# Residues of the MLP input's weights: an accumulating DMA onto the negated rounded half in place of VectorE subtractions

## The chip, the cores and the metric

The kernel runs on one core of a Trainium2 chip. The metric is device time in microseconds of one execution, as the median of several runs. A difference of 0.2% (about 4.5 us) is what a measurement of this kernel can tell from no change.

## The reference, cut to what matters

A trunk of two layers over 256 tokens of width 2048. Each layer has attention (differential and neighbourhood heads) and then a squared-ReLU MLP with 8192 hidden columns. All is float32. The change is in the weights of the first MLP product:

```python
h = rmsnorm(x, mlp_norm[l])
u = jax.nn.relu(jnp.einsum('bsd,df->bsf', h, w_mlp_in[l]))
x = x + jnp.einsum('bsf,fd->bsd', u * u, w_mlp_out[l])
```

## The kernel before, in words

**Split weights.** TensorE multiplies rounded operands (float32r). To keep float32's accuracy, every weight is split into a rounded half and a residue, w = hi + lo with hi = round(w) and lo = w - hi, and so is every activation. A product is then three matmuls into one accumulator: hi x hi, hi x (activation's residue), and lo x hi. The lo half is used by the third alone.

**Slabs.** All weights are packed on the host into slabs of 128 x 2048 floats (1 MB), 192 for each layer, 384 in all, in the order of use. `next_slab` loads one into `raw` (three buffers, on SP's DMA queue, in program order) and splits it in two halves of 128 x 1024: ScalarE (ACT) copies to `whi` (line 130), VectorE (DVE) subtracts to `wlo` (line 131). Each of `whi` and `wlo` has four buffers, which all products of the kernel share.

**Who uses a slab.** `block_product` has the weights as the moving operand, 24 matmuls of 512 columns for each slab (the attention's input, the output projection, the MLP's output: lines 153 to 155). `stationary_product` has the weights as the stationary operand, 48 matmuls of 256 columns for each slab (lines 180 to 182, accumulator `accu`). It serves the neighbourhood heads' q and k (16 slabs a layer, 32 in all) and the MLP's input (64 slabs a layer, 128 in all).

**The MLP.** The hidden columns go in four chunks (`N_CHUNK`). A chunk is an input stage of 16 slabs (`F_PER_CHUNK`), each followed by `rl` = relu (ACT, line 524), `u` = accu x rl (DVE, line 526) and the split of u into `u2T` (ACT line 136, DVE line 137); and then an output stage of 16 slabs, four blocks of four. Two layers make eight such chunks.

**What sets the order.** Each engine runs its instructions in a fixed order, which a scheduler writes from a timeline of its own when the kernel is built; only the loads on SP's queue keep the program's order. What an engine does ahead of TensorE is bounded by the buffers of `raw`, `whi` and `wlo`. GpSimd (POOL) does small things: the scales of the norms (lines 189, 191), the rotary sums (line 250), the biases. It issues no DMA.

Of the kernel before, what the change touches and what calls it, by code (L numbers as in the profile page):

```python
# [11 lines left out]
F32 = mybir.dt.float32  # L12
F32R = mybir.dt.float32r
AF = mybir.ActivationFunctionType
ALU = mybir.AluOpType
# [20 lines left out]
NB = 512  # L36
NEG = -1.0e30
RUN = 5 * RPB_C + GRID_W
# Where a query of column 0 and an even row finds its last neighbour in a head's reversed table.
RPB_FIRST = RPB_HEAD - 1 - (10 * RPB_C + GRID_W - 1 + WIN_C - 1)  # L40
N_CHUNK = 4
F_PER_CHUNK = D_FF // P // N_CHUNK
SLABS = 48 + 16 + 64 + 64
# Column blocks of 512 of the input projection: q, k, v of the differential heads 0-3, then 4-7.
DIFF_BLOCKS = [0, 2, 4, 1, 3, 5]
NA_Q, NA_K, NA_V = 3 * HALF, 4 * HALF, 5 * HALF

# [1 line left out]
def body(ctx, tc, x, x_t, w, gains_in, gains_o, final_g, lam_in, rpb, ident_in, rope_in, mask_in, out):  # L49
# [5 lines left out]
    small = ctx.enter_context(tc.tile_pool(name="small", bufs=4))  # L55
    ps = ctx.enter_context(tc.tile_pool(name="ps", bufs=2, space=PSUM))

# [1 line left out]
    gin = const.tile([P, 2 * DEPTH, NK], F32, name="gin")  # L59
    nc.scalar.dma_start(gin, gains_in)  # L60
    ident = const.tile([P, P], F32, name="ident")
# [3 lines left out]
    xs = [const.tile([P, D], F32, name=f"x{t}") for t in range(NT)]  # L65

    def stream(dst, src):
        """A load on the queue of the weights, in the order of the program."""
        tc.keep_in_program_order(nc.sync.dma_start(dst, src))

    lam_sb = [None]

    def load_table(l):
        """The relative position biases of a layer, from where each query reads its windows."""
        table = act.tile([P, HEADS, RUN + 1], F32, name="table", tag="table", bufs=1)
        for rr in range(P // GRID_W):
            src = bass.AP(tensor=rpb.tensor,
                          offset=rpb.offset + l * HEADS * RPB_HEAD + RPB_FIRST + rr * RPB_C,
                          ap=[[1, GRID_W], [RPB_HEAD, HEADS], [1, RUN]])
            stream(table[rr * GRID_W:(rr + 1) * GRID_W, :, :RUN], src)  # L80
        return table
# [23 lines left out]
    ones = const.tile([P, P], F32, name="ones")  # L105
    nc.vector.memset(ones, 1.0)

# [1 line left out]
    slab_no = [0]  # L109
    x_rest = [None]  # L110

    def next_slab():
        i = slab_no[0]
        slab_no[0] += 1
        raw = wp.tile([P, 2048], F32, name="raw", tag="raw", bufs=3)
        if i == 0:
            for c in range(0, 2048, NB):
                if c == NB:
                    x_rest[0]()
                stream(raw[:, c:c + NB], w[i, :, c:c + NB])  # L120
        else:
            stream(raw, w[i])
        parts = []
        for h in range(2):
            hi = wp.tile([P, 1024], F32R, name="whi", tag="whi", bufs=4)
            lo = wp.tile([P, 1024], F32R, name="wlo", tag="wlo", bufs=4)
            step = NB if i == 0 else 1024
            for c in range(0, 1024, step):
                r = raw[:, h * 1024 + c:h * 1024 + c + step]
                nc.scalar.activation(hi[:, c:c + step], r, AF.Copy)  # L130
                nc.vector.tensor_sub(lo[:, c:c + step], r, hi[:, c:c + step].bitcast(F32))  # L131
            parts.append((hi, lo))
        return parts

# [3 lines left out]
                                       op0=ALU.mult, op1=ALU.subtract)  # L138

    def block_product(n_k, operand, before=None, split_tail=0):  # L140
        """[256, 512] = sum over n_k blocks of 128 of operand(k)^T @ the next slabs. The last
        `split_tail` slabs are held together, so that one tile of tokens ends before the other."""
        acc = [ps.tile([P, NB], F32, name="acc", tag="acc", bufs=4) for _ in range(NT)]
        parts = []
        todo = []

        def one(k, t):
            hi, lo = parts[k // 2]
            c0 = (k % 2) * NB
            a = operand(k)  # L150
            wh, wl = hi[:, c0:c0 + NB], lo[:, c0:c0 + NB]
            ah, al = a[:, 0, t * P:(t + 1) * P], a[:, 1, t * P:(t + 1) * P]
            nc.tensor.matmul(acc[t], ah, wh, start=k == 0, stop=False)  # L153
            nc.tensor.matmul(acc[t], al, wh, start=False, stop=False)  # L154
            nc.tensor.matmul(acc[t], ah, wl, start=False, stop=k == n_k - 1)  # L155

        n_s = n_k // 4
        for s in range(n_s):
            if before is not None:
                before(s)  # L160
            parts += next_slab()
            todo += range(4 * s, 4 * s + 4)
            if s < n_s - split_tail:
                for k in todo:
                    for t in range(NT):
                        one(k, t)
                todo = []
        for t in range(NT):
            for k in todo:
                one(k, t)  # L170
        return acc

    def stationary_product(h_t):
        """[128, 256] = the next slab^T @ normed activations, transposed."""
        parts = next_slab()
        acc = ps.tile([P, S], F32, name="accu", tag="acc", bufs=4)
        for k in range(NK):
            hi, lo = parts[k // 8]
            wh, wl = hi[:, (k % 8) * P:(k % 8 + 1) * P], lo[:, (k % 8) * P:(k % 8 + 1) * P]
            nc.tensor.matmul(acc, wh, h_t[k][:, 0], start=k == 0, stop=False)  # L180
            nc.tensor.matmul(acc, wh, h_t[k][:, 1], start=False, stop=False)  # L181
            nc.tensor.matmul(acc, wl, h_t[k][:, 0], start=False, stop=k == NK - 1)  # L182
        return acc

# [1 line left out]
    def rms_scale(ss, n, width):  # L186
        """(ss / width + EPS) ** -0.5 on [128, n]."""
        v = small.tile([P, n], F32, name="v")
        nc.gpsimd.tensor_scalar(v, ss, 1.0 / width, EPS, op0=ALU.mult, op1=ALU.add)
        r = small.tile([P, n], F32, name="r")  # L190
        nc.gpsimd.tensor_tensor(r, v, mhalf[:, :n], op=ALU.pow)
        return r

    class Norm:
        """RMSNorm of x in pieces: the gain goes into the transposed halves, the scale of
        each token comes out of `scale()` and is applied to the products."""

        def __init__(self, gain):
            self.gain = gain
# [12 lines left out]
            self.h_t[k] = h  # L212

        def take(self, n):
            """Columns n*512... of x are final."""
            for t in range(NT):
                self.squares(n, t)
            for k in range(4 * n, 4 * n + 4):
                pt = ps.tile([P, S], F32, name="tp", tag="tp", bufs=2)
                for t in range(NT):  # L220
                    nc.tensor.transpose(pt[:, t * P:(t + 1) * P], xs[t][:, k * P:(k + 1) * P], ident)  # L221
                self.store(k, pt)
# [5 lines left out]
                self._r[t] = rms_scale(tot, 1, D)  # L228
            return self._r[t]

# [1 line left out]
    def to_sbuf_rope(acc, r, which):  # L232
        """Rotary position of q (which 0) or k (which 1), then transposed: [(m d), head, token]."""
        dst = [act.tile([P, 4, S], F32R, name="qkT", tag="A", bufs=12) for _ in range(2)]
        for t in range(NT):
            nat = work.tile([P, NB], F32, name="nat", tag="nat", bufs=3)
# [41 lines left out]
        return hi, lo  # L278

    def along_free(r):  # L280
        """[128, 256]: r of every token, in all partitions."""
        pb = ps.tile([P, S], F32, name="tp", tag="tp", bufs=2)
        for t in range(NT):
            diag = work.tile([P, P], F32, name="diag", tag="o", bufs=4)
# [4 lines left out]
        return rb  # L289

    def transposed_weights(pr):
        """[128 queries, tile, 256 keys] -> [128 keys, tile, 256 queries] in PSUM."""
        pw = ps.tile([P, NT, S], F32, name="tp", tag="tp", bufs=2)
        for t in range(NT):
            for kt in range(NT):
# [1 line left out]
        return pw  # L297

    def weights_times_v(pr, v, j):
        """pr [128 q, tile, 256 keys] -> [128 q, tile, 128] in PSUM."""  # L300
        pw = transposed_weights(pr)
        wt = work.tile([P, NT, S], F32, name="wT", tag="wT", bufs=3)
        nc.scalar.activation(wt, pw, AF.Copy)
# [5 lines left out]
        return po  # L309

    def to_mix(po, scale, gain):
        """Scaled rows of po, transposed, with the gain, split."""
        o = work.tile([P, NT, HD], F32, name="o", tag="o", bufs=4)
        for t in range(NT):
            nc.vector.tensor_scalar(o[:, t, :], po[:, t, :], scale[:, t:t + 1], None, op0=ALU.mult)
# [110 lines left out]
            else:  # L426
                nc.vector.scalar_tensor_tensor(sl, acc[t], scale[t], sl, op0=ALU.mult, op1=ALU.add)

# [1 line left out]
    norm = Norm(0)  # L430

    def prologue(s):
        """The transposed x comes in beside the first slabs, x itself and the tables behind them."""
        st = act.tile([P, 4, S], F32, name="xT", tag="A", bufs=12)

        def load(k0, k1):
# [10 lines left out]
    for l in range(DEPTH):  # L447
        if l == 0:
            first = [block_product(NK, norm.h_t.__getitem__, before=b) for b in (prologue, load_constants)]
            for t in range(NT):  # L450
                for n in range(4):
                    norm.squares(n, t)
            # lambda, and the sub-norm's gain times 1 - lambda_init
            lq = lam_sb[0].rearrange("p l (a b) d -> p l a b d", b=2)
            prod = work.tile([P, DEPTH, 2, QKD], F32, name="prod", tag="o", bufs=4)
            for i in range(DEPTH):
# [62 lines left out]
        for c in range(N_CHUNK):  # L519
            us = []  # L520
            for f in range(F_PER_CHUNK):
                acc = stationary_product(h_t)
                rl = work.tile([P, S], F32, name="rl", tag="o", bufs=4)
                nc.scalar.activation(rl, acc, AF.Relu)
                u2 = work.tile([P, S], F32, name="u2", tag="o", bufs=4)
# [17 lines left out]
                        nxt.take(n)  # L543
        norm = nxt

# [1 line left out]
    for t in range(NT):  # L547
        r = norm.scale(t)
        for n in (3, 0, 1, 2):
# [27 lines left out]
def _pack_weights(w_in, w_out, w_mlp_in, w_mlp_out):  # L577
    slabs = np.empty((DEPTH, SLABS, P, 2048), np.float32)

    def moving(a):  # L580
        """[K, N] -> [N / 512, K / 512, 128, 4 * 512]"""
        K, N = a.shape
        a = a.reshape(K // NB, 4, P, N // NB, NB).transpose(3, 0, 2, 1, 4)
        return a.reshape(N // NB, K // NB, P, 2048)

    def stationary(a):
        """[2048, N] -> [N / 128, 128, 16 * 128]"""
        return a.reshape(NK, P, -1, P).transpose(2, 1, 0, 3).reshape(-1, P, 2048)

    for l in range(DEPTH):  # L590
# [54 lines left out]
```

## Time and profile before

| what | value |
|---|---|
| median of three runs | 2261.7 us (2261.6 to 2261.77) |
| span of the profiled execution | 2259.7 us |
| PE busy (matmul) | 2244.5 us, 99% |
| DVE busy | 1296.5 us, 57% |
| ACT busy | 1063.4 us, 47% |
| POOL busy | 91.9 us, 4% |
| SP's weight queue, share of 16 DMA engines | 50.8%, 411.40 MB |

The profiled execution's span lies 2.0 us below the median; what is added up from its rows is set against 2259.7 us and then moved by these 2.0 us. The page says in 40 slices how busy each engine is: PE shows 9 in all but the first and the last, DVE 5 to 6, ACT 3 to 6, DMA mostly 4 to 5.

### The profile page before, as it was taken

Reading aid. Unit: us, or ns where it says so; the run is one execution under the profiler, and the core shown is the slowest. Engines: PE = TensorE matmul, PEld = TensorE weight load, DVE = VectorE, ACT = ScalarE, POOL = GpSimd, SP = SyncE. Lnnn points to the kernel's source line nnn. Section 1 sums busy time; section 2 is a strip of 40 time slices with the busy share of each in tenths; the row PEclk is TensorE's granted clock in tenths of the full one; section 3 lists DMA queues with packets and bytes.
Section 4 is the critical chain, followed back from the end, with each engine's and each line's share of the span. In section 5 each row is a group of like instructions: output and inputs, shape, how many; then the busy total and the mean of one; then the engine's idle time right before and its main releaser. Section 6 shows DMA issues by size and latency. Waiting matters only on the chain.

```text
span 2259.7 us, 33741 instructions
## 1 busy us (share of the span) xinstructions
PE 2244.5 (99%) x13904; PEld 2019.3 (89%) x13904; DVE 1296.5 (57%) x1615; ACT 1063.4 (47%) x1579; POOL 91.9 (4%) x136
## 2 busy tenths in 40 slices
PE   8999999999999999999999999999999999999998
PEld 7889998998998898899888899989989989988986
DVE  6656666655555555555566666665555555555554
ACT  6556454543444444344445564545434434444443
POOL 1111000000000000000010110000000000000000
PEclk9999999999999999999999999999999999999999
DMA  9453445555555545555654434455555555455553
GB/s 326 149 186 135 173 161 186 184 179 196 187 187 186 190 183 189 198 178 185 202 188 162 168 140 170 179 191 180 187 188 186 186 193 192 179 197 189 186 188 131
DMA packets 61306, 414.63 MB, mean 183 GB/s; under 512 B 7008, under 2 KB 9184, under 8 KB 11872
## 3 DMA queue, kind: packets, MB, share of 16 engines
q1 hardware_dynamic: 60720, 411.40, 50.8%
q8 instruction: 109, 1.79, 0.3%
q10 hardware_dynamic: 432, 1.08, 0.2%
q14 instruction: 45, 0.37, 0.0%
HBM read 410.35 MB, written 2.10 MB: 183 GB/s over the span
## 4 chain that ended last, share of the span: by engine, by line
PE 99%; DMA 0%; DVE 0%; ACT 0%; SPq 0%; issue 0%; POOL 0%; ACTq 0%; POOLq 0%
PE acc L155 18%; PE acc L153 18%; PE acc L154 18%; PE accu L180 14%; PE accu L182 14%; PE accu L181 14%; PE tp L307 1%; PE tp L296 1%; PE tp L221 0%; PE sc L343 0%; DMA raw<-in_w 0%; PE tp L257 0%; PE sc L345 0%; PE sc L344 0%; PE tp L412 0%; PE sc L387 0%
## 5 line engine op out<-in xcount | busy, mean ns | idle before, releaser
L131 DVE TENSOR_TENSOR wlo<-raw,whi 128x1024 fp32r<-128x1024 f32 (+1 forms) x770 | 945.7, 1229 | 848.0 <-ACT whi L130 841.4
L130 ACT ACTIVATE whi<-raw 128x1024 fp32r<-128x1024 f32 (+1 forms) x770 | 814.7, 1059 | 1055.5 <-PE acc L154 548.9
L181 PE MATMUL accu<-hT,whi 128*128 128x256 f32 x2560 | 726.0, 284 | 0.0
L182 PE MATMUL accu<-hT,wlo 128*128 128x256 f32 x2560 | 724.6, 283 | 0.0
L180 PE MATMUL accu<-hT,whi 128*128 128x256 f32 x2560 | 724.0, 283 | 0.0
L181 PEld LDWEIGHTS accu<-hT,whi 128*128 128x128 f32 x2560 | 491.5, 192 | 0.5
L180 PEld LDWEIGHTS accu<-hT,whi 128*128 128x128 f32 x2560 | 490.8, 192 | 0.8
L182 PEld LDWEIGHTS accu<-hT,wlo 128*128 128x128 f32 x2560 | 491.4, 192 | 0.0
L154 PE MATMUL acc<-whi,u2T 128*128 128x512 f32 x1024 | 399.2, 390 | 0.0
L153 PE MATMUL acc<-whi,u2T 128*128 128x512 f32 x1024 | 398.7, 389 | 0.0
L155 PE MATMUL acc<-wlo,u2T 128*128 128x512 f32 x1024 | 398.5, 389 | 0.0
L155 PEld LDWEIGHTS acc<-wlo,u2T 128*128 128x128 f32 x1024 | 192.3, 188 | 39.7
L153 PEld LDWEIGHTS acc<-whi,u2T 128*128 128x128 f32 x1024 | 192.3, 188 | 39.6
L154 PEld LDWEIGHTS acc<-whi,u2T 128*128 128x128 f32 x1024 | 192.3, 188 | 39.3
L153 PE MATMUL acc<-whi,hT 128*128 128x512 f32 x512 | 202.7, 396 | 6.0 <-ACT whi L130 6.0
L154 PE MATMUL acc<-whi,hT 128*128 128x512 f32 x512 | 203.0, 397 | 0.0
L155 PE MATMUL acc<-wlo,hT 128*128 128x512 f32 x512 | 199.4, 395 | 0.1
L153 PEld LDWEIGHTS acc<-whi,hT 128*128 128x128 f32 x512 | 96.9, 189 | 26.3 <-ACT whi L130 6.2
L155 PEld LDWEIGHTS acc<-wlo,hT 128*128 128x128 f32 x512 | 96.7, 189 | 20.3 <-DVE wlo L131 0.5
L154 PEld LDWEIGHTS acc<-whi,hT 128*128 128x128 f32 x512 | 96.9, 189 | 19.7
L154 PE MATMUL acc<-whi,mix 128*128 128x512 f32 x256 | 100.7, 393 | 0.0
L153 PE MATMUL acc<-whi,mix 128*128 128x512 f32 x256 | 100.7, 393 | 0.0
(117 smaller groups left out, 1331.9 us busy)
## 6 DMA issues: line engine op xcount, KB each, us to landing
raw<-in_w SPq DMA_DIRECT2D x383, 1024.0 KB, 4.8
x<-in_x SPq DMA_DIRECT2D x2, 1024.0 KB, 9.7
out<-xg SPq DMA_DIRECT2D x8, 256.0 KB, 3.1
table<-in_rpb SPq DMA_DIRECT2D x4, 438.0 KB, 11.5
xT<-in_x_t SPq DMA_DIRECT2D x3, 512.0 KB, 9.5
raw<-in_w SPq DMA_DIRECT2D x4, 256.0 KB, 5.4
gb<-in_final_g ACTq DMA_DIRECT2D x2, 512.0 KB, 5.7
xT<-in_x_t SPq DMA_DIRECT2D x2, 256.0 KB, 3.5
```

The costliest lines, as they stand in the source:

```text
L130: nc.scalar.activation(hi[:, c:c + step], r, AF.Copy)
L131: nc.vector.tensor_sub(lo[:, c:c + step], r, hi[:, c:c + step].bitcast(F32))
L153: nc.tensor.matmul(acc[t], ah, wh, start=k == 0, stop=False)
L154: nc.tensor.matmul(acc[t], al, wh, start=False, stop=False)
L155: nc.tensor.matmul(acc[t], ah, wl, start=False, stop=k == n_k - 1)
L180: nc.tensor.matmul(acc, wh, h_t[k][:, 0], start=k == 0, stop=False)
L181: nc.tensor.matmul(acc, wh, h_t[k][:, 1], start=False, stop=False)
L182: nc.tensor.matmul(acc, wl, h_t[k][:, 0], start=False, stop=k == NK - 1)
L296: nc.tensor.transpose(pw[:, kt, t * P:(t + 1) * P], pr[:, t, kt * P:(kt + 1) * P], ident)
L307: nc.tensor.matmul(po[:, t, :], wt[:, kt, t * P:(t + 1) * P], v[:, kt, j * HD:(j + 1) * HD], start=kt == 0, stop=kt == NT - 1)
```

## The change

In the 128 slabs of the MLP's input, and there alone, DVE makes no residue. ACT makes a second pass over `raw`, with scale -1, into the `wlo` buffer, which gives the negated rounded half; then a DMA issued by POOL reads the same 128 x 1024 weights from HBM once more and adds them onto that buffer, which leaves w - hi. `whi` gets a fifth buffer and `wlo` a fifth and a sixth; the space for descriptors of POOL's DMAs is set to 4096 bytes a partition. Comments and docstrings are removed, which moves line numbers by up to four.

```diff
-    def next_slab():
+    def next_slab(residue_by_dma=False):
...
-            hi = wp.tile([P, 1024], F32R, name="whi", tag="whi", bufs=4)
-            lo = wp.tile([P, 1024], F32R, name="wlo", tag="wlo", bufs=4)
+            hi = wp.tile([P, 1024], F32R, name="whi", tag="whi", bufs=5)
+            lo = wp.tile([P, 1024], F32R, name="wlo", tag="wlo", bufs=6)
             step = NB if i == 0 else 1024
             for c in range(0, 1024, step):
                 r = raw[:, h * 1024 + c:h * 1024 + c + step]
                 nc.scalar.activation(hi[:, c:c + step], r, AF.Copy)
-                nc.vector.tensor_sub(lo[:, c:c + step], r, hi[:, c:c + step].bitcast(F32))
+                if residue_by_dma:
+                    nc.scalar.activation(lo, r, AF.Copy, scale=-1.0)
+                    nc.gpsimd.dma_start(lo, w[i, :, h * 1024:(h + 1) * 1024], accum_op=ALU.add)
+                else:
+                    nc.vector.tensor_sub(lo[:, c:c + step], r, hi[:, c:c + step].bitcast(F32))
             parts.append((hi, lo))
...
-    def stationary_product(h_t):
+    def stationary_product(h_t, residue_by_dma=False):
...
-        parts = next_slab()
+        parts = next_slab(residue_by_dma)
...
-                acc = stationary_product(h_t)
+                acc = stationary_product(h_t, True)
...
-    nc = bacc.Bacc("TRN2", target_bir_lowering=False, num_devices=1)
+    nc = bacc.Bacc("TRN2", target_bir_lowering=False, num_devices=1, dynamic_dma_scratch_size=4096)
```

ACT's order in the middle of an MLP input stage before, two slabs long (`rl` belongs to a slab whose 48 matmuls have ended, `whi` to slabs still to come):

```order
L524 ACTIVATE rl<-accu 128x256
L130 ACTIVATE whi<-raw 128x1024
L136 ACTIVATE u2T<-u_7586 128x256
L130 ACTIVATE whi<-raw 128x1024
L524 ACTIVATE rl<-accu 128x256
L130 ACTIVATE whi<-raw 128x1024
L136 ACTIVATE u2T<-u_7652 128x256
L130 ACTIVATE whi<-raw 128x1024
```

The same engine and place in the changed kernel:

```order
L528 ACTIVATE rl<-accu 128x256
L132 ACTIVATE wlo<-raw 128x1024
L140 ACTIVATE u2T<-u_6290 128x256
L130 ACTIVATE whi<-raw 128x1024
L132 ACTIVATE wlo<-raw 128x1024
L130 ACTIVATE whi<-raw 128x1024
L528 ACTIVATE rl<-accu 128x256
L132 ACTIVATE wlo<-raw 128x1024
```

Two passes `wlo` have come in for each slab. Counted over the whole order, when ACT reaches the `rl` of slab s, the `wlo` passes of all halves up to the fifth after slab s stand ahead of it (in the stage's first slabs of a layer up to the seventh), and the pass of the sixth stands right behind it.

POOL's order around the first layer's MLP before (`v`, `r` and `rr` are the scales of the norm):

```order
L189 TENSOR_SCALAR v<-tot 128x1 x2
L191 TENSOR_TENSOR r<-v,mhalf 128x1 x2
L189 TENSOR_SCALAR v<-tot 128x1
L191 TENSOR_TENSOR r<-v,mhalf 128x1
L189 TENSOR_SCALAR v<-tot 128x1
L508 TENSOR_TENSOR rr_4041<-r 128x1
L191 TENSOR_TENSOR r<-v,mhalf 128x1
L508 TENSOR_TENSOR rr_4043<-r 128x1
```

And in the changed kernel:

```order
L193 TENSOR_SCALAR v<-tot 128x1 x2
L195 TENSOR_TENSOR r<-v,mhalf 128x1 x2
L133 DMA wlo<-in_w 128x1024 x6
L193 TENSOR_SCALAR v<-tot 128x1
L195 TENSOR_TENSOR r<-v,mhalf 128x1
L193 TENSOR_SCALAR v<-tot 128x1
L512 TENSOR_TENSOR rr_4041<-r 128x1
L195 TENSOR_TENSOR r<-v,mhalf 128x1
L512 TENSOR_TENSOR rr_4043<-r 128x1
L133 DMA wlo<-in_w 128x1024 x122
```

Six of a layer's 128 accumulating DMAs stand ahead of the scales of the norm, the other 122 behind them in one row, with nothing between them.

## Rows read from the trace of the kernel before

**Rows 1.** The page: busy us (share of the span) and instructions of each engine.

```profile
PE 2244.5 (99%) x13904; PEld 2019.3 (89%) x13904; DVE 1296.5 (57%) x1615; ACT 1063.4 (47%) x1579; POOL 91.9 (4%) x136
```

**Rows 2.** The page: the chain that ended last, shares of the span by engine.

```profile
PE 99%; DMA 0%; DVE 0%; ACT 0%; SPq 0%; issue 0%; POOL 0%; ACTq 0%; POOLq 0%
```

**Rows 3.** Timeline of ACT in the first chunk: start us, us, instruction, idle before.

```profile
458.12 0.37 ACT L524 ACTIVATE rl<-accu 128x256 f32<-128x256 f32 x1
460.02 1.06 ACT L130 ACTIVATE whi<-raw 128x1024 fp32r<-128x1024 f32 x1 [1.53 <-issue]
460.99 0.40 ACT L136 ACTIVATE u2T<-u 128x256 fp32r<-128x256 f32 x1
462.91 1.06 ACT L130 ACTIVATE whi<-raw 128x1024 fp32r<-128x1024 f32 x1 [1.53 <-PE accu L181]
463.88 0.37 ACT L524 ACTIVATE rl<-accu 128x256 f32<-128x256 f32 x1
```

**Rows 4.** Windows: the first chunk's input stage (412.00 to 504.60 us).

```profile
core 0: us, PE busy (x) PEld busy (x) DVE busy (x) ACT busy (x) POOL busy (x), PEclk, DMA share, GB/s
412.00:504.60 92.60, 92.60 (x769) 92.34 (x768) 50.85 (x70) 45.17 (x70) 1.82 (x6) 1.00 0.52 182
```

**Rows 5.** Groups of DVE in that stage, 424.0 to 504.6 us: busy us, mean ns.

```profile
L131 DVE TENSOR_TENSOR wlo<-raw,whi 128x1024 fp32r<-128x1024 f32 x30 | 36.7, 1225 | 38.0 <-ACT whi L130 37.8
L137 DVE SCALAR_TENSOR_TENSOR u2T<-u,u2T 128x256 fp32r<-128x256 f32 x15 | 6.3, 419 | 0.0
L526 DVE TENSOR_TENSOR u<-accu,rl 128x256 f32<-128x256 f32 x15 | 6.3, 417 | 0.0
```

**Rows 6.** Groups of ACT in the same window.

```profile
L130 ACT ACTIVATE whi<-raw 128x1024 fp32r<-128x1024 f32 x30 | 31.8, 1060 | 43.7 <-PE accu L181 26.8 <-issue 16.9
L136 ACT ACTIVATE u2T<-u 128x256 fp32r<-128x256 f32 x15 | 6.0, 400 | 0.0
L524 ACT ACTIVATE rl<-accu 128x256 f32<-128x256 f32 x16 | 5.9, 367 | 0.0
```

**Rows 7.** SP's queue, waits over the whole span: us, times, longest.

```profile
SPq L69 <- DVE wlo L131: 1158.9, 220, 10.5
SPq L69 <- DVE u L526: 709.3, 124, 7.3
```

**Rows 8.** Timeline of SP's queue near the start: start us, us of issue.

```profile
16.79 0.43 SPq L69 DMA_DIRECT2D ident<-in_ident_in  x1
...
20.28 0.33 SPq L69 DMA_DIRECT2D raw<-in_w  x1
```

**Rows 9.** The page, groups of POOL: busy us, mean ns.

```profile
L250 POOL TENSOR_TENSOR nat<-nat,tmp 128x512 f32<-128x512 f32 x16 | 26.9, 1681 | 82.9 <-DVE tmp L247 78.1 <-DVE tot L227 4.4 <-PE acc L154 0.2
L191 POOL TENSOR_TENSOR r<-v,mhalf 128x2 f32<-128x2 f32 (+1 forms) x30 | 19.8, 664 | 2.0
```

**Rows 10.** DMA in the first 40 us, 40 slices of 1 us; queue: packets, MB, share.

```profile
DMA  0287899999999999999999999999999999999999
GB/s 0 48 299 190 252 324 266 356 440 446 418 397 451 438 406 414 426 418 451 410 393 387 452 408 401 418 434 442 401 393 410 430 348 180 160 161 211 228 224 219
```

**Rows 11.** DMA in the first chunk's input stage, 412.0 to 504.6 us.

```profile
q1 hardware_dynamic: 2304, 16.78, 51.1%
```

**Rows 12.** The page, DMA issues: count, KB each, median us to landing.

```profile
raw<-in_w SPq DMA_DIRECT2D x383, 1024.0 KB, 4.8
x<-in_x SPq DMA_DIRECT2D x2, 1024.0 KB, 9.7
...
table<-in_rpb SPq DMA_DIRECT2D x4, 438.0 KB, 11.5
```

**Rows 13.** The page: PE's longest idle group, last figures.

```profile
L153 PE MATMUL acc<-whi,hT 128*128 128x512 f32 x512 | 202.7, 396 | 6.0 <-ACT whi L130 6.0
```

## The prediction

> **What bounds the kernel now.** I read the page's busy times first, then the chain that ended last, and then the stage that the change touches. PE is busy for 2244.5 of 2259.7 us [rows 1], and the chain is PE to 99% [rows 2]. So only 15 us of the span are not matmuls, and work taken from another engine shortens nothing by itself. In the first chunk's input stage PE is busy in all of its 92.60 us [rows 4]. Two `rl`, one of each slab, start 5.76 us apart, at 458.12 and 463.88 [rows 3]: this is PE's pace of a slab, 2.88 us for a half. DVE has the most work after PE, but waits for ACT's `whi`, and ACT waits for PE to give buffers back [rows 5, 6]. The subtractions that go are thus hidden behind PE today. What the reader should ask is whether what replaces them stays hidden too, at 5.76 us a slab.
>
> **What goes.** 256 subtractions of 1225 ns [rows 5], 314 us of DVE. None of it is on the path: worth 0.
>
> **ACT's second pass.** It shows no row of its own, but it is the `whi` copy with another scale, 1060 ns [rows 6]. A slab then takes ACT 4 x 1.06 + 0.37 + 0.40 = 5.01 us of PE's 5.76: hidden, with 0.75 us to spare. Without that cover, each further microsecond a slab costs 128 us in all.
>
> **The lead of a residue.** A third of PE's matmuls of a half read `wlo`, from the half's start. By ACT's new order, the pass of the sixth half after a slab stands right behind the slab's `rl`, and six buffers are just enough for that. PE has five halves to do in the meantime, 5 x 2.88 = 14.4 us. Of these `rl` and the pass take 0.37 + 1.06, which leaves 12.97 us for POOL's issue and the DMA until it has landed. Loads of 1 MB land in 4.8 us alone and in 9.7 us with others queued before them, the table's in 11.5 [rows 12]. So the time of a single DMA is hidden, as long as DMAs don't pile up. The change adds this wait on POOL: each DMA waits for ACT's pass, and queued behind it are only further DMAs of the same kind, since 122 of them stand in one row; the norm's scales that stand behind the first six aren't wanted until the output stage. SP's loads of `raw` now wait for ACT's pass and not for DVE's subtraction; they waited for DVE 1868 us in total [rows 7], which says that the buffers, not the queue, hold them back today.
>
> **POOL's issue.** Before has no DMA from POOL. The nearest rows are SP's issues of 0.33 to 0.43 us [rows 8] from below and POOL's own operations of 0.66 and 1.68 us [rows 9] from above. At two a slab, anything up to 2.88 us hides; I take 0.
>
> **The DMA engines** are where I see the cost. A load: with several queued, the first 40 us run at a steady 387 to 452 GB/s, mean 420 over 24 slices [rows 10], so 1 MB (1.049e6 bytes) takes 1.049 / 0.420 = 2.50 us. In the input stage the loads' packets take 51.1% of the engines' time [rows 11], 2.9 us of 5.76, because a lone load starts and ends unevenly; I use 2.50. The accumulating DMA reads another 1 MB a slab from HBM, reads 1 MB of `wlo`, and writes 1 MB. No row shows such a DMA. The bounds: as cheap as a plain load of the same bytes, 2.50 us a slab; and three legs one after another, read, read, write, each as long as a load, 7.50. In between lies 5.00, two reads that share the engine's reading side while the writing runs beside them. I take 5.00, since a plain load has one read and one write that run beside each other at 420 GB/s, and the row is for that.
>
> The Trainium skill ("Collectives: The Full Stack", section "Part 3: Why 7× under link rate — side-by-side accounting") puts an add in the DMA engines at half a copy's rate, since the two sources are read through one ring, with 1.93 as the measured ratio. By that an estimate is 1.93 x 2.50 = 4.83 us, and the sum below would be +136 in place of +157 us. No run here shows it yet.
>
> **The sum for a chunk.** The residues run five halves ahead, so the engines have the stage's 16 x 5.76 = 92.2 us and 14.4 us before it, 106.6 us, in which PE takes 18.5 slabs. Their work in this time: 18.5 loads x 2.50 = 46.3 us, since the loads keep their own lead for the output stage, and 16 x 5.00 = 80.0 us: 126.3 us. PE comes out 19.7 us late in each chunk. The output stage has no accumulating DMAs (its residues stay with DVE), so the next chunk starts with the full lead again and nothing is carried over. 8 x 19.7 = +157 us on 2259.7, so 2417 for the profiled execution and, with the 2.0 us to the median, 2419. What is late then is `wlo` through the DMA, never ACT.
>
> By the bounds: 2.50 gives 46.3 + 40.0 = 86.3 us, under 106.6, so nothing; 7.50 gives 166.3, +59.7 a chunk, +478 in all. The point from which the change costs anything is (106.6 - 46.3) / 16 = 3.77 us a slab, 1.5 loads.
>
> **The rivals.**
>
> *The DMA fits: no change, 2262.* It holds if the adding costs up to 3.77 us a slab. For it: a plain load needs 2.50, and the engines are idle for half of the stage [rows 11]. Against it: 3 MB are to be read and 2 MB written each 5.76 us, which is 546 GB/s of reading, more than the 452 of the best slice [rows 10]. It stands if reading `wlo` doesn't count against the rate of the loads.
>
> *The add runs one leg after another: 2739.* 7.50 us a slab as above, +478. For it: the sum must have been read before it can be written. Against it: a load's reading and writing run beside each other [rows 10], and an add could do the same from one row to the next. Dearer still than three legs (10 us would give +798) I can't exclude.
>
> *POOL or the latency becomes the bound, not the engines' rate.* This ends slower too, by one mechanism: each DMA needs POOL's issue, and they go one by one. It decides from 2.88 us of issue; at 3.5 us, twice POOL's longest row, a slab takes 7.0 us and 128 x 1.24 = +159, 2420: the same time as the forecast, told apart by POOL's busy share. ACT belongs here as well: were each of its six operations of a slab 0.2 us apart, 6.2 us a slab would give +56.
>
> *Faster.* DVE being free could shorten only what PE waits for. Its longest idle group is 6.0 us in the first blocks [rows 13], for a `whi` of ACT, before the first MLP. A fifth buffer of `whi` could take that away at best: 2256. Against it: that early the loads themselves run at the full 420 GB/s [rows 10], and more buffers don't make these faster.
>
> **How the numbers follow.** The adding between 3.77 and 6.25 us a slab, so the forecast with up to +317: 0.40. Above that, with the three legs: 0.22. POOL or ACT: 0.10. It fits: 0.25. Faster: 0.03. So slower by over 0.2% (4.5 us, about what a measurement of this kernel can tell from no change) 0.72, within 0.2% 0.25, faster 0.03. The likeliest is 2419. The range starts at 2257, the lower edge of no change, which leaves 0.03 below, and ends at 2760, past the three legs, which leaves some 0.15 above. Of the slower cases alone it would be 2300 to 2760.
>
> **What would show it.** If I am right, the changed profile has a second large DMA queue with POOL's 256 DMAs, and in the input stages the engines' share is near full; from `rl` to `rl` the first slabs keep 5.76 us and the later ones take the engines' 2.50 + 5.00 = 7.5; PE's idle time stands at line 186 (the `wlo` matmul), put down to a DMA; and the output stages last as long as before. If POOL is the bound, POOL is busy through the stage and the DMA share stays below full. If it fits, the pace stays at 5.76 and PE at 99%. I'd be wrong in kind if PE lost time in the output stages, or ACT were the one that PE waits for.

## The result, and the profile after

The changed kernel takes 2478.4 us (median of four runs, 2475.5 to 2480.7) against 2261.7 us: a ratio of 1.0958, with a 95% interval of 1.0942 to 1.0973. It is 217 us slower; 157 us were forecast (2419 us). The profiled execution's span is 2476.3 us, 216.6 us over that of before.

The page of the changed kernel: first the busy times, which answer to [rows 1]; then the DMA queues (packets, MB, share of 16 engines); then the chain that ended last, which answers to [rows 2].

```profile
PE 2295.4 (93%) x13904; PEld 2037.3 (82%) x13904; DVE 1001.6 (40%) x1359; ACT 1303.8 (53%) x1835; POOL 315.5 (13%) x392
...
q1 hardware_dynamic: 60720, 411.40, 45.2%
q0 software_dynamic: 36864, 134.23, 27.4%
...
PE 62%; DMA 28%; issue 7%; ACT 1%; POOL 1%; DVE 0%; POOLq 0%; ACTq 0%; SPq 0%
DMA wlo<-in_w 28%; PE acc L157 15%; PE acc L158 15%; PE acc L159 15%; PE accu L186 5%; PE accu L184 4%; PE accu L185 4%; POOL wlo L133 1%; PE tp L311 1%; PE tp L300 1%; ACT wlo L132 1%; ACT whi L130 1%; DVE wlo L135 0%; PE sc L347 0%; PE tp L225 0%
```

DVE has lost 295 us and ACT has gained 240, and neither has more than 1% of the chain. What is new there is above all the DMA that adds onto `wlo`, with 28% of the span. The groups and the issues on the same page say the same (busy us, mean ns, idle before; then KB each and us to landing; the loads answer to [rows 12]):

```profile
L186 PE MATMUL accu<-hT,wlo 128*128 128x256 f32 x2560 | 741.7, 292 | 165.4 <-DMA wlo<-in_w 165.3
...
L133 POOL DMA_DIRECT2D wlo<-in_w x256 | 221.4, 865 | 1306.0 <-ACT wlo L132 1031.5
...
raw<-in_w SPq DMA_DIRECT2D x383, 1024.0 KB, 4.9
wlo<-in_w POOLq DMA_DIRECT2D x256, 512.0 KB, 17.0
```

PE stands idle for 165 us at the matmul that reads the residue, always for that DMA, which takes 17.0 us to land. POOL needs 0.865 us to issue one. PE's waits for it (us, times, longest):

```profile
PE accu L186 <- DMA wlo<-in_w: 165.3, 125, 4.0
```

The other 51 us of the loss stand in PE's busy time, which went from 2244.5 to 2295.4 us. In the rows these matmuls last 0.28 us and start 0.12 us apart, so a part of each wait is counted as busy; how much of the 51 us that is, and how much the granted clock (last section), wasn't taken apart.

The pace is read from ACT's `rl` in the second chunk's input stage, as in [rows 3] (timeline: start us, us):

```profile
626.59 0.37 ACT L528 ACTIVATE rl<-accu 128x256 f32<-128x256 f32 x1
636.76 0.36 ACT L528 ACTIVATE rl<-accu 128x256 f32<-128x256 f32 x1
...
659.25 0.36 ACT L528 ACTIVATE rl<-accu 128x256 f32<-128x256 f32 x1
666.76 0.36 ACT L528 ACTIVATE rl<-accu 128x256 f32<-128x256 f32 x1
674.28 0.36 ACT L528 ACTIVATE rl<-accu 128x256 f32<-128x256 f32 x1
```

From slab to slab it is 7.51 and 7.52 us, where it was 5.76; the second slab of the stage, the first that has to wait, takes 10.2 (the last takes 10.0, for another reason that comes further down). In eight slabs of the first chunk's stage the DMA engines look like this (468.60 to 528.68 us, 40 slices, then packets, MB, share; the queue of the loads answers to [rows 11]):

```profile
DMA  9999999999999999999999999999999999999999
...
q0 software_dynamic: 2317, 8.41, 70.5%
q1 hardware_dynamic: 1137, 8.27, 34.2%
```

They have no free slice, and the adds take twice the loads' share for the same bytes. (The two shares sum to 105%: packets of two queues overlap a little on an engine.) The output stage after it, 540 to 625 us (columns as in [rows 4]), is whole: PE is busy in all of its 85.00 us.

```profile
540.00:625.00 85.00, 85.00 (x397) 71.28 (x396) 38.12 (x37) 39.96 (x40) 5.15 (x6) 1.00 0.64 212
```

### The profile page after: what moved, and what is told of

Same layout as the page of the kernel before. It is cut to its first block, busy times and chain, and to the rows that moved or that the text cites. A ratio compares the mean times of both kernels' runs of the same rounds, so it can differ in the third digit from the quotient of the medians.

```text
span 2476.3 us, 34045 instructions
## 1 busy us (share of the span) xinstructions
PE 2295.4 (93%) x13904; PEld 2037.3 (82%) x13904; DVE 1001.6 (40%) x1359; ACT 1303.8 (53%) x1835; POOL 315.5 (13%) x392
## 4 chain that ended last, share of the span: by engine, by line
PE 62%; DMA 28%; issue 7%; ACT 1%; POOL 1%; DVE 0%; POOLq 0%; ACTq 0%; SPq 0%
DMA wlo<-in_w 28%; PE acc L157 15%; PE acc L158 15%; PE acc L159 15%; PE accu L186 5%; PE accu L184 4%; PE accu L185 4%; POOL wlo L133 1%; PE tp L311 1%; PE tp L300 1%; ACT wlo L132 1%; ACT whi L130 1%; DVE wlo L135 0%; PE sc L347 0%; PE tp L225 0%
## 5 line engine op out<-in xcount | busy, mean ns | idle before, releaser
L186 PE MATMUL accu<-hT,wlo 128*128 128x256 f32 x2560 | 741.7, 292 | 165.4 <-DMA wlo<-in_w 165.3
L135 DVE TENSOR_TENSOR wlo<-raw,whi 128x1024 fp32r<-128x1024 f32 (+1 forms) x514 | 631.4, 1230 | 552.9 <-ACT whi L130 548.8
L133 POOL DMA_DIRECT2D wlo<-in_w x256 | 221.4, 865 | 1306.0 <-ACT wlo L132 1031.5
L530 DVE TENSOR_TENSOR u<-accu,rl 128x256 f32<-128x256 f32 x128 | 54.2, 424 | 580.5 <-ACT rl L528 580.5
L132 ACT ACTIVATE wlo<-raw 128x1024 fp32r<-128x1024 f32 x256 | 267.4, 1045 | 1.6 <-DMA raw<-in_w 1.6
```

The source lines that it names most:

```text
L132: nc.scalar.activation(lo, r, AF.Copy, scale=-1.0)
L133: nc.gpsimd.dma_start(lo, w[i, :, h * 1024:(h + 1) * 1024], accum_op=ALU.add)
L530: nc.vector.tensor_mul(u2, acc, rl)
```

## The experiments

Four theories were set against each other. A: the DMA engines are full in the input stages, because an adding DMA takes them twice as long as a copy. B: any DMA that POOL issues is that slow, or the rounding to float32r makes it so. C: the landing time of 17 us, through six buffers, sets the pace. D: the buffers or ACT's second pass cost something.

**The buffers alone.** The new numbers of buffers and the descriptor space stay, the residues are VectorE's again.

```diff
-                acc = stationary_product(h_t, True)
+                acc = stationary_product(h_t)
```

> The buffers and the descriptor space of the change (whi 5, wlo 6, 4096 bytes), but the residues by VectorE as before. Theory A (the DMA engines are full, because an adding DMA reads twice), B (any DMA issued by POOL, or its rounding to float32r, is that slow) and C (17 us of landing through six buffers set the pace): 2262 us, PE idle as in the kernel before. Theory D (the buffers or ACT's second pass cost something themselves): anything up to 2478.

Measured: 2261.5 us, ratio 1.000 (0.9989 to 1.0011). The buffers neither cost nor gain.

**ACT's second pass alone.**

```diff
                     nc.scalar.activation(lo, r, AF.Copy, scale=-1.0)
-                    nc.gpsimd.dma_start(lo, w[i, :, h * 1024:(h + 1) * 1024], accum_op=ALU.add)
```

> The changed kernel without its DMAs: the residue stays the negated rounded half, the addition of the weights is left out. Theories A, B and C: 2262 us and 5.76 us from rl to rl, since ACT's second pass is hidden. D: slower by the part that is ACT's; were ACT the bound, over 5.76 us a slab.

Measured: 2261.8 us, ratio 1.000 (0.9989 to 1.0012). ACT is busy for 1302.8 us, as in the changed kernel, and all of the added work hides. D is out; the loss is in the DMAs.

**Plain copies in place of the adds.**

```diff
-                    nc.gpsimd.dma_start(lo, w[i, :, h * 1024:(h + 1) * 1024], accum_op=ALU.add)
+                    nc.gpsimd.dma_start(lo, w[i, :, h * 1024:(h + 1) * 1024])
```

> The changed kernel with POOL's DMAs as plain copies: the weights overwrite the negated half and the addition is left out; as many DMAs of the same bytes, also to float32r, issued by the same engine after the same waits. A: 2.5 + 2.5 = 5.0 us of the engines a slab, under PE's 5.76, so 2262 us, landing well under 17 us. B: 7.5 us a slab and 2478 us. C: 2262 if a copy lands in less than 13 us, else between.

Measured: 2266.8 us, ratio 1.0022 (1.0011 to 1.0033). The same bytes by the same engine after the same waits cost 5 us, not 217. From its page, the queues and the landing:

```profile
q1 hardware_dynamic: 60720, 411.40, 50.0%
q0 software_dynamic: 36864, 134.23, 17.2%
...
wlo<-in_w POOLq DMA_DIRECT2D x256, 512.0 KB, 7.2
```

B is out: it is the adding. That not all hides (PE waits 3.5 us for these DMAs) shows how little room is left even for a copy.

**Five buffers of `wlo`.**

```diff
-            lo = wp.tile([P, 1024], F32R, name="wlo", tag="wlo", bufs=6)
+            lo = wp.tile([P, 1024], F32R, name="wlo", tag="wlo", bufs=5)
```

> The changed kernel with five buffers of wlo in place of six. A: the engines stay full, so the pace stays at 7.5 us a slab and the landing falls by one half, from 17 to some 13.3 us; time 2478 to 2501 (the lead at each stage's start is up to a half of 2.9 us shorter, eight times). C: the landing stays at 17 us and the pace goes to 2 x (17.1 + 5.5) / 5 = 9.0 us a slab, some 2650 us.

Measured: 2477.4 us (two runs), ratio 1.0953 (1.0922 to 1.0985). The landing fell to 13.4 us and the pace stayed (its issues, and two `rl` of the second chunk):

```profile
wlo<-in_w POOLq DMA_DIRECT2D x256, 512.0 KB, 13.4
...
682.19 0.36 ACT L528 ACTIVATE rl<-accu 128x256 f32<-128x256 f32 x1
689.69 0.36 ACT L528 ACTIVATE rl<-accu 128x256 f32<-128x256 f32 x1
```

C is out: with one DMA less in flight each waits one place less in the queue, 3.6 us, and 7.50 us a slab remains. The 17 us are the queue before a full resource, not a latency. The time lies at the low end of the expectation's 2478 to 2501; what that says of the lead comes with the last experiment.

**The add by itself.** Four kernels with the buffers and the VectorE residues of before, in which POOL issues the 256 DMAs beside the work, 128 in a row from the start of each layer's MLP, onto tiles that nobody reads. They differ in the DMA alone:

```diff
+                if residue_by_dma:
+                    nc.gpsimd.dma_start(beside[beside_no[0] % 3], w[i, :, h * 1024:(h + 1) * 1024], accum_op=ALU.add)
+                    beside_no[0] += 1
```

> The cost of the add by itself. The buffers and the VectorE residues of the kernel before; beside them POOL issues the change's 256 DMAs onto three float32 tiles that nobody reads, 128 in a row from the start of each layer's MLP. A (two reads): the engines' time for 1 MB of adding 5.0 to 5.3 us, as in the changed kernel. If rounding to float32r is the cost: about 2.5 us, half of it. Time 2262 us or a little more (loads come late while the DMAs run).

> The same with the three tiles in float32r, as wlo is. A: as the float32 add, 5.0 to 5.3 us of the engines for 1 MB. If rounding costs: more than the float32 add.

> The same with plain copies from HBM onto the float32 tiles. A: about 2.5 us of the engines for 1 MB, half of the add. B (POOL's DMAs are slow of themselves): 5 us, as the add.

> The same add with a constant float32 tile in SBUF as the source, and two tiles in turn (a third has no room): no second read of HBM. If the second read of HBM is what is short: about 2.5 us for 1 MB, or clearly less than the add from HBM. If it is the engines' own work on two sources: 5 us as from HBM.

All four take 2261 to 2262 us (one run each): PE isn't held up by DMAs that it doesn't wait for, though the loads' landing goes from 4.8 us to between 8.6 and 9.0 beside the adds (4.9 beside the copies). The same 60 us of the first input stage, 440 to 500 us, in the four (POOL's queue: packets, MB, share): the float32 add,

```profile
q0 software_dynamic: 1879, 6.84, 57.2%
```

the add onto float32r,

```profile
q0 software_dynamic: 1885, 6.87, 57.5%
```

the copy,

```profile
q0 software_dynamic: 3224, 11.72, 50.6%
```

and the add from a tile in SBUF:

```profile
q0 software_dynamic: 1700, 6.18, 51.9%
```

Share x 60 us / MB x 1.049 is the engines' time for a slab's megabyte: 5.26, 5.27, 2.72 and 5.28 us. By these shares an add costs 1.94 copies. With the loads (46.8% beside the first add, 48.3% beside the copy) the shares sum to 104% in the one case and 99% in the other; scaled to the time that passed, the ratio is 1.85. So it is about two, and not known to the second digit. Rounding adds nothing, and the second read of HBM is not what is short, since the add whose two sources both lie in SBUF costs the same. That leaves the engines' own work on two sources; whether it is the reading of the second or the adding itself, these runs don't tell apart.

The Trainium skill ("Collectives: The Full Stack", section "Part 3: Why 7× under link rate — side-by-side accounting") has 1.93 for an add with two sources against a copy, between cores; the 1.85 to 1.94 here agree with that, for one core and with either source.

**A part of the adds.** If the engines' room decides, there is a threshold; if each DMA costs its share, the loss goes with their number.

```diff
-                if residue_by_dma:
+                if residue_by_dma and h == 0:
```

> The changed kernel with the DMA's add for the first half of each slab alone; VectorE subtracts for the second. A with the add's time as now read from the traces (5.28 us of the engines for 1 MB, 2.57 for a load): 2.57 + 2.64 = 5.21 us a slab, under PE's 5.76, so 2262 us. If every adding DMA costs its share wherever there is room (217 us / 256 each): 2370 us.

Measured: 2265.5 us, ratio 1.0019 (1.0009 to 1.0029). And three of four:

```diff
-                if residue_by_dma:
+                if residue_by_dma and (h == 0 or i % 2):
```

> The DMA's add for three halves of every four, VectorE for the fourth. A: 2.57 + 3.96 = 6.53 us a slab in the stage's steady part, against PE's 5.76; over a stage 18 x 2.57 + 16 x 3.96 = 109.6 us of the engines against 92.2 + 11.3 us of PE, 6.1 us late in each of eight, 2311 us. Each DMA its share: 2424 us.

Measured: 2337.0 us, ratio 1.0326 (1.0309 to 1.0343). Half of the adds cost 4 us of the whole's 217, three quarters cost 75: a threshold, as A has it. With half of them even these 4 us stand in the first chunk of each layer (174.3 and 174.4 us from its first `rl` to that of the second chunk, 172.3 before); the second and third chunks of both layers take 179.2 us as before. PE's waits in the two kernels (us, times, longest), half and then three quarters:

```profile
PE accu L186 <- DMA wlo<-in_w: 3.4, 2, 1.7
```

```profile
PE accu L186 <- DMA wlo<-in_w: 52.3, 48, 2.4
```

The 75 us are more than the 49 of the expectation; the next section has the term that was left out.

**Four buffers of `whi`.**

```diff
-            hi = wp.tile([P, 1024], F32R, name="whi", tag="whi", bufs=5)
+            hi = wp.tile([P, 1024], F32R, name="whi", tag="whi", bufs=4)
```

> The changed kernel with four buffers of whi, as before the change, in place of five. If the residues' lead at a stage's start hangs on whi (ACT's pass for a wlo stands behind the whi of the same half, which waits for a whi buffer): one half less of lead, 2.7 us in each of eight stages, 2500 us, at an unchanged 7.5 us a slab. If the lead hangs on wlo's six buffers alone: 2478 us.

Measured: 2493.5 us, ratio 1.1025 (1.1009 to 1.1042), 15 us over the changed kernel. The first add of the second chunk in POOL's timeline, the changed kernel and then this one (PE starts the stage at 619.74 and at 621.95 us):

```profile
608.41 0.86 POOL L133 DMA_DIRECT2D wlo<-in_w  x1 [92.15 <-ACT wlo L132]
```

```profile
613.35 1.80 POOL L133 DMA_DIRECT2D wlo<-in_w  x2 [94.98 <-ACT wlo L132]
```

The lead at the stage's start is 11.3 us with five `whi` and 8.6 us with four, and so it is in all six stages that follow an output stage of their layer. Eight times 2.7 us would be 22 us, and 15 show in the time. But the kernel with five `wlo` starts its first add of this stage here, 8.6 us before PE too (620.60 us):

```profile
611.99 0.86 POOL L133 DMA_DIRECT2D wlo<-in_w  x1 [91.05 <-ACT wlo L132]
```

It lost nothing by that (2477.4 us). So one buffer fewer takes 2.7 us off the lead in either pool. That `whi` alone sets the lead isn't shown, and lead that is lost need not show in the time.

## Why the prediction was right, and where it was off

**What goes, and what hides.** The subtractions were worth nothing, and ACT's second pass, the lead's single DMA and POOL's issue hid, as written: the pass alone ran in 2261.8 us, and POOL's 0.865 us is far under the 2.88 us at which it would have decided.

**The DMA engines** are the bound, as written. The reason given, two reads on the engine's reading side, isn't shown: the runs have an add at about two copies and don't tell its second read from its adding. The value taken between the bounds, two reads, 5.00 us a slab, gave 2.50 + 5.00 = 7.5 us from `rl` to `rl`, and 7.51 was measured. So this term is not what made the 60 us by which the forecast was short. The engines' shares give 2.57 and 5.29 us a slab in that stage, but these sum to more than the time that passed; scaled to it they are 2.45 and 5.04.

**The sum for a chunk** is the step that was too small. From the first `rl` of the second chunk to that of the third there were 205.6 us (626.59 to 832.16) and 179.2 before, so PE comes out 26.4 us late, not 19.7. By the sum, PE is late by the engines' time from the first add to the last landing, less the lead, less what PE does in between: 126.3 - 14.4 - 92.2 = 19.7. In the trace of the second chunk the first add is issued at 608.41 us and the last lands at 736.26 (its semaphore), 127.8 us later, and all three terms are off:

- The lead was taken as 14.4 us, five halves, from the six `wlo` buffers and ACT's order in the middle of a stage. The stage's first add starts 11.3 us before PE [the POOL row above]. In ACT's order each pass for a `wlo` stands behind the `whi` of the same half, and there are five `whi`. This is 3.1 us a chunk. One buffer fewer in either pool shortens it further; what would lengthen it no run shows.
- PE's work at the end was taken as done when the last residue has landed. At 736.26 us PE still has 46 of the stage's 768 matmuls to do, 5.5 us at 0.12 us each, and has done 16 of the output stage in their place, 3.6 us: 1.9 us.
- The engines took 127.8 us and not 126.3, though they moved 17.8 slabs of loads in them (18.69 MB) and not 18.5: 1.5 us. With 2.50 us for a load, 5.2 us of them are left for each slab of adds.

19.7 + 3.1 + 1.9 + 1.5 = 26.2 of 26.4 us. This accounts for the chunk as it ran; it doesn't test each term by itself. With five `wlo` the lead is 2.7 us shorter still, and yet a chunk takes 205.0 us: the last landing comes 126.3 us after the first add, and 24 matmuls of the stage are then left. Nor does PE wait for the last landing, as the sum has it. Its last wait of the stage ends 5.8 us sooner:

```profile
730.43 0.38 PE L186 MATMUL accu<-hT,wlo 128*128 128x256 f32 x1 [1.12 <-DMA wlo<-in_w]
```

The expectation for three quarters of the adds left out PE's work at the end as well: there 29 matmuls of the second chunk's stage, 3.5 us, are left at the last landing. With the 2.9 us of a half, eight times, its 2311 become 2334 us, where 2337 was measured, and 2329 in the one of four runs whose mean granted clock was 0.999 (0.995 or 0.996 in the others).

Over the whole kernel 216.6 / 8 is 27.1 us a chunk; the first chunk of a layer differs, since its first slabs run beside the norm's transposes.

**The first slabs** don't keep 5.76 us, as the prediction had it: one slab runs freely, then comes a wait (10.2 us for the second slab). The lead was pictured as slack that is used up over the stage, but the engines are full from the first add on, and loads and adds share them at once, so that the third half already lands late (PE waits 2.3 us for it). The sum over the stage isn't touched by that.

At the other end some work is moved. In the fixed order of PE, matmuls of the output stage stand between those of the last slabs (timeline of the changed kernel):

```profile
733.03 0.28 PE L186 MATMUL accu<-hT,wlo 128*128 128x256 f32 x1
733.15 0.40 PE L159 MATMUL acc<-wlo,u2T 128*128 128x512 f32 x1
```

So the last `rl` comes 10.0 us after the one before it, and the next stage then follows 4.9 us sooner than before (87.9 us from the last `rl` to the next first, where there were 92.8). A look at the input stage alone, 117.7 us from the first `rl` to the last where there were 86.5, would put the loss 4.9 us too high.

**The rivals.** That the DMA fits needed an add of at most 3.77 us a slab; the copy, with 2.72, falls on that side and runs in 2266.8 us, and so do half of the adds. Three legs one after another would have shown 10 us a slab. POOL or ACT as the bound: excluded above. Faster: PE's longest idle group of the first blocks is there as before, 6.4 us and 5.9 with the buffers alone, against the 6.0 of [rows 13]; the fifth `whi` doesn't touch it.

## What to carry to other kernels

An adding DMA took the DMA engines about as long as two copies of its bytes, with the source in HBM or in SBUF; add it to the loads of the stage in which it runs, not to an average over the kernel, and compare with that stage's time. Below the threshold it is all but free here, above it the excess is on the path, in every stage anew. Where engines prefetch into several pools of buffers, read the lead at the stage's start from the order there, not from the size of one pool in the middle of a stage, and count what the waiting engine still has to do when the last piece lands.

## What the runs showed of the hardware

- POOL's issue of a DMA of 128 rows of 4 KB takes 0.865 us when it adds and 0.53 us when it copies (the two kernels' groups of POOL). The first of the two lies within the bounds of [rows 8] and [rows 9].
- PE's granted clock falls for a moment at the start of some stages, where PE has just waited: 0.69 over 835 to 840 us, which is part of the time at the lower of its two levels.

```profile
835.00:840.00 5.00, 5.00 (x32) 4.89 (x32) 0.00 (x0) 2.01 (x2) 0.16 (x1) 0.69 1.05 270
```

In the changed kernel it costs nothing that can be seen: the third chunk, to which this row belongs, takes 205.3 us from first `rl` to first `rl`, and the second, in which the clock stays full, 205.6. PE waits for residues there from slab to slab, and a slower PE can hide in these waits. With three quarters of the adds it isn't hidden: the second chunk there keeps the full clock and the third does not (columns as in [rows 4]), and the third takes 3.2 us more.

```profile
605.70:793.83 188.13, 181.11 (x1154) 164.75 (x1153) 67.67 (x80) 100.49 (x122) 20.82 (x24) 1.00 0.82 245
793.83:985.12 191.29, 184.12 (x1154) 167.70 (x1153) 67.68 (x80) 100.54 (x121) 20.82 (x24) 0.98 0.81 243
```
